# Packing the first five weight tiles by tile of x, and loading x between the weights, at the start of a two-block transformer kernel

## The chip, the core and the metric

The kernel runs on one core of a Trainium2 chip. The metric is the time of one execution on the device in microseconds. Three executions before the change took 1213.05, 1207.31 and 1213.48 us (median 1213.05).

## What is computed

Two blocks follow each other on x of 256 tokens by 1024 channels, in fp32. The change concerns the first lines of the first block alone:

```python
h = rms_norm(x, norm_mix_g[l])          # x * rsqrt(mean(x*x) + 1e-6) * g
proj = h @ w_in[l]
qa, ka, va, qc, kc, vc, rx, rgate, gates = jnp.split(proj, offs, axis=-1)
ya = moba_attention(qa..., ka..., va...)
```

`qa`, `ka` and `va` are 512 columns each. Behind them come a recurrence, a second attention, gated merges, a feed-forward part, and then a second block of two layers, whose code the change leaves as it is.

## The kernel before

**Layout.** x lies transposed: 8 tiles of 128 channels by 256 tokens (`x[:, k]`, k = 0 to 7). A weight tile is 128 x 128 fp32 (64 KB). An output tile of 128 columns needs eight weight tiles, one for each tile of x. All weights of the program are packed on the host, in the order of their use, into one stream that `_plan` writes down (L63 and after); `Stream` (L147) reads it in chunks of eight tiles (512 KB) into six raw buffers. In `_plan` each of the eight `qa` and `ka` output tiles is a run of eight weight tiles, so chunk 0 holds all of `qa` tile 0, chunk 1 all of `qa` tile 1, and so on.

**Splitting.** Products are made from a high and a low part, both in the format that TensorE reads. For a chunk, ScalarE casts to `whi` (L186) and VectorE subtracts to `wlo` (L187); there are five buffers of each. Chunk 0 is split in pieces of 2, 3 and 3 tiles, chunks 1 and 2 in halves. Each weight tile then takes three matmuls of 256 columns (`mm3`, L343 to L345): high with high, high with the low part of the moving operand, low with high.

**The start.** `load_x` (L262) loads two tiles of x at a time. SyncE issues x 0 and 1, two tiles of chunk 0, x 2 and 3, the other six tiles, x 4 to 7, and then chunks 1 to 5 and the tables. Thirteen warm-up matmuls on `ones` (L328) run meanwhile.

**The first projections** go through `seam` (L476) with nothing before it (`prev` is empty). The norm's factor for a token can be applied after the product, so the first `NSTART` = 5 output tiles (four of `qa`, one of `ka`) are computed on x times the gain alone: `zh` and `zl` (registers R0 and R1, L509 and L510). Tile by tile, all eight k are done before the next begins. After the third tile (`i == 2`) the norm is finished: `norm.add` sums squares (L393, L396 on ScalarE, L405 on GpSimd and once on VectorE), `stats` (L418) adds over channels with a matmul against `ones`, VectorE and ScalarE make the reciprocal root (L428, L471 to L474, result `n_r`), and `apply` writes the normalised input for all later tiles: product with `n_r` (L457), high part `hh` (L464, ScalarE), low part `hl` (L465, VectorE). The five tiles are scaled by `n_r` when they leave PSUM (L532). The other `ka` tiles, and all that follows, read `hh` and `hl`: in this document "the key tiles" are these three, `ka` 1 to 3. Behind them `tokens` computes `va` (VA, L759 to L761).

**What sets the order.** A scheduler orders each engine's instructions when the program is built; each engine then runs its own list in order. The lists are shown below where the change moves them.

Of the kernel before, what the change touches and what calls it, by code (L numbers as in the profile page):

```python
# [10 lines left out]
F32 = mybir.dt.float32  # L11
F32R = mybir.dt.float32r
# [54 lines left out]
def _plan():  # L67

    runs = []

    def cols(name, layer, col, nk=8, nc=1):
        runs.append((name, layer, nk, col, nc))

    for c in (QA, KA):
        for m in range(4):
            cols("w_in", 0, c + m * P)
    cols("w_in", 0, VA, 8, 4)
    for m in range(8):
        cols("w_in", 0, RX + m * P)
        if m > 1:  # L80
            runs.append(("rg", 0, 2, m - 2, 1))
        cols("w_in", 0, GT + m * P)
    for c in (QC, KC):
        for m in range(4):
            cols("w_in", 0, c + m * P)
            if c == QC and m < 2:
                runs.append(("rg", 0, 2, 6 + m, 1))
    cols("w_in", 0, VC, 8, 4)
    for m in range(8):
        cols("w_in", 0, RGT + m * P)  # L90
    for m in range(8, 16 + GLEAD):
        cols("w_in", 0, GT + m * P)
    for kind, m in WEAVE:
        if kind == "gate":
            cols("w_in", 0, GT + (16 + m) * P)
        else:
            cols("w_branch_a", 0, m * P, 4)
            cols("w_branch_b", 0, m * P, 8)
            cols("w_branch_c", 0, m * P, 4)
    for m in range(8):  # L100
        cols("w_out", 0, m * P)
    for j in range(FT):
        cols("ffn_up", 0, j * P)
        cols("ffn_up", 0, (j + FT) * P)
    for m in range(8):
        cols("ffn_down", 0, m * P, FT)
    for l in range(2):
        for c in (XC2, GB2):
            for m in range(2):
                cols("w_in_2", l, c + m * P)  # L110
        cols("w_in_2", l, K2)
        cols("w_in_2", l, V2)
        for m in range(4):
            cols("q2", l, m)
        for c in (POOL2, GC2):
            for m in range(2):
                cols("w_in_2", l, c + m * P)
        for n in range(GLEAD2):
            if n == POOLAT:
                runs.append(("pool2", l, 2, 0, 1))  # L120
            cols("w_in_2", l, GT2 + (n % 3 * 8 + n // 3) * P)
        for kind, m in WEAVE2:
            if kind == "gate":
                cols("w_in_2", l, GT2 + (m % 3 * 8 + m // 3) * P)
            else:
                cols("w_branch_a_2", l, m * P, 2)
                cols("w_branch_b_2", l, m * P, 4)
                cols("w_branch_c_2", l, m * P, 2)
        for m in range(8):
            cols("w_o_2", l, m * P)  # L130
        for j in range(FT):
            cols("w_up_2", l, j * P)
            cols("w_up_2", l, (j + FT) * P)
        for m in range(8):
            cols("w_down_2", l, m * P, FT)
    at, t = {}, 0
    for r in runs:
        at[(r[0], r[1], r[3])] = t
        t += r[2] * r[4]
    return runs, at, t  # L140
# [6 lines left out]
class Stream:  # L147
# [13 lines left out]
    def load(self):  # L161
        c = self.loads
        if c >= NCH:
            return
        n = min(CT, NTILES - c * CT) * P
        t = self.pool.tile([P, CT * P], F32, name="raw", tag="raw", bufs=NRAW)
        src = self.src[c * CT * P * P:c * CT * P * P + P * n].rearrange("(p n) -> p n", p=P)
        cut = 2 * P if c == 0 else n
        self.nc.sync.dma_start(t[:, :cut], src[:, :cut])
        if cut < n:  # L170
            self.between[0]()
            self.nc.sync.dma_start(t[:, cut:n], src[:, cut:])
            self.between[1]()
        self.raw[c] = t
        self.loads += 1

# [59 lines left out]
def _build(tc, ctx, ap):  # L236
# [22 lines left out]
    par = const("par", [P, P_N])  # L259
    nc.scalar.dma_start(par[:, :8], ap["par"][:, :8])  # L260

    def load_x(k):  # L262
        nc.sync.dma_start(x[:, k:k + 2], ap["xT"][k * P:(k + 2) * P].rearrange("(k p) t -> p k t", p=P))

    load_x(0)
    W = Stream(nc, wp, ap["wst"], (lambda: load_x(2), lambda: (load_x(4), load_x(6))))
    nc.sync.dma_start(par[:, 8:], ap["par"][:, 8:])
    sinks = const("sinks", [P, 16])
    nc.sync.dma_start(sinks, ap["row"][None, 256:272].to_broadcast([P, 16]))
# [7 lines left out]
    def cs(name):  # L277
        o, w = C_OFF[name]
        return cst[:, o:o + w]
# [52 lines left out]
    def reg(i, dt=F32, shape=(P, NT, S)):  # L332

        return cp.tile(list(shape), dt, name=f"R{i}", tag=f"R{i}", bufs=1)
# [141 lines left out]
    def seam(prev, evac, norm, nxt, zreg, nahead=NAHEAD):  # L476

        ahead, rest = nxt[:nahead], nxt[nahead:]
        width = S + 2 if norm.ln else S
        if nxt:
            zh, zl = (reg(i, F32R, (P, NT, width)) for i in zreg)
            if norm.ln:
                for i, c in enumerate((norm.g, norm.b)):
                    split(zh[:, :, S + i], zl[:, :, S + i], c)
        for m in range(NT):
            if prev:  # L490
                t0, nk, rhs, _ = prev[m]
                if nk == 8 and m < 3:
                    if m == 0:
                        W.begin(t0, 3 * nk)
                        first = [ps() for _ in range(3)]
                        for ks in (range(6), range(6, 8)):
                            for q, (t, _, r, _) in zip(first, prev):
                                for k in ks:
                                    wh, wl = W.get(t + k)
                                    mm3(q[:, :S], wh, wl, r[0][:, k], r[1][:, k], k == 0, k == 7)  # L500
                    p = first[m]
                else:
                    W.begin(t0, nk)
                    p = ps()
                    group(p[:, :S], t0, nk, rhs)
                evac(m, p[:, :S])
            if nxt:
                g = norm.g[:, m:m + 1]
                A.activation(zh[:, m, :S], x[:, m], AF.Copy, scale=g)  # L509
                V.scalar_tensor_tensor(zl[:, m, :S], x[:, m], g, zh[:, m, :S].bitcast(F32), op0=OP.mult, op1=OP.subtract)  # L510
            if prev:
                norm.add(m, not nxt)
        if not nxt:
            norm.stats(True)
            norm.finish(zreg)
            return
        out = []
        for i, mt in enumerate(ahead):
            W.begin(mt["t0"], 8)
            p = ps()  # L520
            out.append(p)
            for k in range(8):
                wh, wl = W.get(mt["t0"] + k)
                mm3(p[:, :width], wh, wl, zh[:, k], zl[:, k], k == 0, k == 7)
            if i == (0 if prev else 2):
                for m in range(0 if prev else NT):
                    norm.add(m)
                norm.stats()
                norm.apply()
        for mt, p in zip(ahead, out):  # L530
            t = mt["into"] if "into" in mt else wrk()
            V.tensor_tensor(t, p[:, :S], norm.rstd, op=OP.mult)  # L532
            if norm.ln:
                gb = tmp("n_gb", [P, 2], 2)
                A.copy(gb, p[:, S:width])
                u = wrk()
                A.activation(u, norm.nmr, AF.Identity, scale=gb[:, 0:1], bias=gb[:, 1:2])
                G.tensor_add(t, t, u)
            if "evac" in mt:
                mt["evac"](t)  # L540
        for i in range(0, len(rest), 2):
            pair = rest[i:i + 2]
            W.begin(pair[0]["t0"], 8 * len(pair))
            pn = [ps() for _ in pair]
            for k in range(8):
                for mt, p in zip(pair, pn):
                    wh, wl = W.get(mt["t0"] + k)
                    mm3(p[:, :S], wh, wl, hh[:, k], hl[:, k], k == 0, k == 7)
            for mt, p in zip(pair, pn):
                mt["evac"](p[:, :S])  # L550

    def to_hi_lo(dst, i, scale=None):
        return lambda p: split(dst[0][:, i], dst[1][:, i], p, scale)

# [164 lines left out]
    def rope_tables():  # L719
# [12 lines left out]
        for sc in (65536.0, 1.0):  # L732
# [9 lines left out]
        V.tensor_scalar(sinT, sinT, cs("sgn"), None, op0=OP.mult)  # L742

    sc64 = 64 ** -0.5
    seam([], None, n0, [dict(t0=AT["w_in", 0, QA + m * P], nk=8, rhs=HX, evac=to_hi_lo(qa, m, cs("qsa")[:, m:m + 1])) for m in range(4)]
         + [dict(t0=AT["w_in", 0, KA + m * P], nk=8, rhs=HX, evac=to_hi_lo(ka, m)) for m in range(2)], (0, 1), NSTART)
    with tc.issue_after(n0.done.ins):
        small()
    phase([dict(t0=AT["w_in", 0, KA + m * P], nk=8, rhs=HX, evac=to_hi_lo(ka, m)) for m in range(2, 4)])

    def tokens(t0, dst):
        def go():
# [419 lines left out]
```

## Time and profile before

| | |
|---|---|
| median of three executions | 1213.05 us |
| lowest and highest | 1207.31 and 1213.48 us |
| the profiled execution | 1208.3 us, of it the span 1206.3 us |
| mean granted TensorE clock over the span | 0.986 of full speed |
| TensorE matmul busy | 97% of the span |
| VectorE, ScalarE, GpSimd busy | 79%, 63%, 20% |
| weights moved | 395 transfers of 512 KB among 212.61 MB in all |

Times in the profile count from the start of the span. A row of the timeline has start, duration, engine, line of the kernel, operation, output and inputs, and in brackets the idle time of the engine before it and what ended it. "PE" is TensorE, "DVE" VectorE, "ACT" ScalarE, "POOL" GpSimd, and "SPq" the queue of SyncE from which transfers are issued. A share of busy time of PE is not a share of its peak, as matmuls overlap.

### The profile page before, as it was taken

How to read it: one execution, taken by the hardware profiler on the slowest of the kernel's cores; microseconds unless marked ns; L12 is line 12 of the kernel's file. 1: busy time of each engine (PE TensorE's matmuls, PEld its weight loads, DVE VectorE, ACT ScalarE, POOL GpSimd, SP SyncE). 2: the span in 40 equal slices, each digit the busy share in tenths (PEclk: the TensorE clock that was granted, in tenths of full speed). 3: DMA queues.
4: the chain of work that ended last, by engine and by line, in shares of the span. 5: the costliest groups of instructions: out<-in, count | busy, mean ns of one | idle time of the engine just before them, and what ended most of it. 6: DMA issues, size and time to landing. Idle time of an engine off the chain costs nothing.

```text
span 1206.3 us, 25236 instructions
## 1 busy us (share of the span) xinstructions
PE 1165.5 (97%) x9928; PEld 1146.3 (95%) x9928; DVE 956.2 (79%) x1767; ACT 763.7 (63%) x1391; POOL 245.0 (20%) x233
## 2 busy tenths in 40 slices
PE   8999999999999999999999999999999998999895
PEld 8999899999999999999998999999999998999895
DVE  7989886797988856886789988757995888977754
ACT  7678566756767645676557766556776565855542
POOL 2022020001122200120023222222420042222122
PEclk9999999999999999999999999999999998999898
DMA  7654445475466665545554566664455554565541
GB/s 284 224 168 155 166 143 168 127 229 189 148 212 202 196 207 192 162 154 175 184 184 142 165 210 203 209 193 148 151 189 177 185 166 135 155 203 185 189 141 35
DMA packets 60486, 212.61 MB, mean 176 GB/s; under 512 B 6864, under 2 KB 9296, under 8 KB 60368
## 3 DMA queue, kind: packets, MB, share of 16 engines
q1 hardware_dynamic: 60080, 210.88, 54.3%
q8 instruction: 77, 1.26, 0.4%
q10 hardware_dynamic: 288, 0.14, 0.1%
q14 instruction: 41, 0.34, 0.1%
HBM read 209.94 MB, written 1.05 MB: 175 GB/s over the span
## 4 chain that ended last, share of the span: by engine, by line
PE 65%; DVE 17%; ACT 9%; issue 5%; POOL 3%; DMA 0%; SPq 0%; POOLq 0%; ACTq 0%; DVEq 0%
PE ps L344 20%; PE ps L343 20%; PE ps L345 20%; DVE wlo L187 7%; ACT whi L186 4%; POOL wrk L929 2%; DVE R L510 1%; DVE wrk L923 1%; DVE wrk L922 1%; ACT a_lg L580 1%; PE ps L563 1%; PE ps L760 1%; PE ps L761 1%; PE ps L759 1%; DVE wrk L454 1%
## 5 line engine op out<-in xcount | busy, mean ns | idle before, releaser
L187 DVE TENSOR_TENSOR wlo<-raw,whi 128x1024 fp32r<-128x1024 f32 (+1 forms) x401 | 496.3, 1240 | 118.5 <-ACT whi L186 113.1
L343 PE MATMUL ps<-hh,whi 128*128 128x256 f32 x1912 | 536.5, 281 | 5.1 <-ACT hh L461 3.6
L344 PE MATMUL ps<-hl,whi 128*128 128x256 f32 x1912 | 532.0, 279 | 3.2 <-DVE hl L462 3.1
L186 ACT CAST whi<-raw 128x1024 fp32r<-128x1024 f32 (+1 forms) x401 | 414.6, 1038 | 186.8 <-PE ps L344 135.5
L345 PE MATMUL ps<-hh,wlo 128*128 128x256 f32 x1912 | 531.3, 278 | 0.6 <-DVE wlo L187 0.4
L343 PEld LDWEIGHTS ps<-hh,whi 128*128 128x128 f32 x1912 | 361.6, 189 | 8.3 <-ACT hh L461 4.0
L344 PEld LDWEIGHTS ps<-hl,whi 128*128 128x128 f32 x1912 | 362.1, 190 | 4.4 <-DVE hl L462 4.0
L345 PEld LDWEIGHTS ps<-hh,wlo 128*128 128x128 f32 x1912 | 361.1, 189 | 1.0 <-DVE wlo L187 1.0
L343 PE MATMUL ps<-R,whi 128*128 128x256 f32 (+1 forms) x1180 | 330.2, 281 | 6.8 <-ACT R L355 3.8
L344 PE MATMUL ps<-R,whi 128*128 128x256 f32 (+1 forms) x1180 | 329.5, 280 | 5.2 <-DVE R L510 3.5
L345 PE MATMUL ps<-R,wlo 128*128 128x256 f32 (+1 forms) x1180 | 327.9, 279 | 0.4 <-DVE wlo L187 0.2
L343 PEld LDWEIGHTS ps<-R,whi 128*128 128x128 f32 x1180 | 223.6, 190 | 9.0 <-ACT R L355 4.5
L344 PEld LDWEIGHTS ps<-R,whi 128*128 128x128 f32 x1180 | 223.5, 189 | 7.5 <-DVE R L510 4.9
L345 PEld LDWEIGHTS ps<-R,wlo 128*128 128x128 f32 x1180 | 223.1, 189 | 1.3 <-DVE wlo L187 1.2
L929 POOL TENSOR_TENSOR wrk<-wrk 128x256 f32<-128x256 f32 x63 | 82.9, 1316 | 238.6 <-DVE wrk L923 150.3
L355 ACT CAST R<-wrk 128x256 fp32r<-128x256 f32 x89 | 36.0, 407 | 117.5 <-POOL wrk L929 95.3
L405 POOL TENSOR_TENSOR n_sq<-n_sq,n_q 128x256 f32<-128x256 f32 x42 | 39.5, 941 | 169.1 <-ACT n_q L396 167.9
L922 DVE SCALAR_TENSOR_TENSOR wrk<-ps,par,wrk 128x255 f32<-128x255 f32 x120 | 56.6, 476 | 17.3 <-ACT wrk L921 17.3
L356 DVE TENSOR_TENSOR R<-wrk,R 128x256 fp32r<-128x256 f32 x89 | 38.9, 440 | 27.0 <-ACT R L355 26.9
L923 DVE SCALAR_TENSOR_TENSOR wrk<-ps,par,wrk 128x254 f32<-128x254 f32 x120 | 57.1, 477 | 1.6
L611 POOL TENSOR_SCALAR a_lg<-a_lg,a_r 128x256 f32<-128x256 f32 x24 | 25.3, 1056 | 113.1 <-DVE a_r L586 60.9
L509 ACT ACTIVATE R<-x,par 128x256 fp32r<-128x256 f32 x48 | 23.8, 507 | 27.8 <-DVE x L889 16.0
(225 smaller groups left out, 1088.7 us busy)
## 6 DMA issues: line engine op xcount, KB each, us to landing
raw<-in_wst SPq DMA_DIRECT2D x395, 512.0 KB, 4.0
x<-in_xT SPq DMA_DIRECT2D x4, 256.0 KB, 4.8
out_y<-x SPq DMA_DIRECT2D x3, 256.0 KB, 2.2
cst<-in_cst SPq DMA_DIRECT2D x1, 406.0 KB, 8.9
raw<-in_wst SPq DMA_DIRECT2D x1, 384.0 KB, 5.5
par<-in_par SPq DMA_DIRECT2D x1, 312.5 KB, 8.5
raw<-in_wst SPq DMA_DIRECT2D x1, 256.0 KB, 2.7
out_y<-x SPq DMA_DIRECT2D x2, 128.0 KB, 2.0
```

The costliest lines, as they stand in the source:

```text
L186: self.nc.scalar.copy(hi[:, a:b], w[:, a:b])
L187: self.nc.vector.tensor_sub(lo[:, a:b], w[:, a:b], hi[:, a:b].bitcast(F32))
L343: T.matmul(out, sh, mh, start=first, stop=False, skip_group_check=skip)
L344: T.matmul(out, sh, ml, start=False, stop=False, skip_group_check=skip)
L345: T.matmul(out, sl, mh, start=False, stop=last, skip_group_check=skip)
L355: A.copy(hi, src)
L356: V.tensor_sub(lo, src, hi.bitcast(F32))
L405: e.tensor_add(self.sq, self.sq, q)
L611: (G if i else V).tensor_scalar(pe[:, c], pe[:, c], r[:, i:i + 1], None, op0=OP.mult)
L922: V.scalar_tensor_tensor(y[:, 1:], p[:, :S - 1], pr(cw, 44 + i), y[:, 1:], op0=OP.mult, op1=OP.add)
L923: V.scalar_tensor_tensor(y[:, 2:], p[:, :S - 2], pr(cw, i), y[:, 2:], op0=OP.mult, op1=OP.add)
L929: G.tensor_tensor(y, held.pop(j), y, op=OP.mult)
```

## The change

The first five output tiles' weights are one run of 40 tiles now, packed by k: the five tiles for x tile 0, the five for x tile 1, and so on. A new function `begin` replaces the call of `seam`: for each k it makes `zh` and `zl` of that tile of x, and then five times three matmuls, one set for each output tile, into five PSUM tiles at once. `norm.add(k)` follows each k; `stats` and `apply` follow the eighth. The loads of x come apart: x 0, five tiles of chunk 0, x 1, the other three, chunk 1, x 2 and 3, chunk 2, x 4 and 5, chunk 3, x 6 and 7, chunks 4 and 5. The three key tiles go through `phase`, one after the other.

```diff
--- before.py
+++ after.py
@@ -71,9 +71,9 @@
     def cols(name, layer, col, nk=8, nc=1):
         runs.append((name, layer, nk, col, nc))
 
-    for c in (QA, KA):
-        for m in range(4):
-            cols("w_in", 0, c + m * P)
+    cols("w_in", 0, QA, 8, NSTART)
+    for m in range(NSTART, 8):
+        cols("w_in", 0, QA + m * P)
     cols("w_in", 0, VA, 8, 4)
     for m in range(8):
         cols("w_in", 0, RX + m * P)
@@ -165,12 +165,13 @@
         n = min(CT, NTILES - c * CT) * P
         t = self.pool.tile([P, CT * P], F32, name="raw", tag="raw", bufs=NRAW)
         src = self.src[c * CT * P * P:c * CT * P * P + P * n].rearrange("(p n) -> p n", p=P)
-        cut = 2 * P if c == 0 else n
+        cut = NSTART * P if c == 0 else n
         self.nc.sync.dma_start(t[:, :cut], src[:, :cut])
         if cut < n:
             self.between[0]()
             self.nc.sync.dma_start(t[:, cut:n], src[:, cut:])
-            self.between[1]()
+        elif c < len(self.between):
+            self.between[c]()
         self.raw[c] = t
         self.loads += 1
 
@@ -259,11 +260,11 @@
     par = const("par", [P, P_N])
     nc.scalar.dma_start(par[:, :8], ap["par"][:, :8])
 
-    def load_x(k):
-        nc.sync.dma_start(x[:, k:k + 2], ap["xT"][k * P:(k + 2) * P].rearrange("(k p) t -> p k t", p=P))
-
-    load_x(0)
-    W = Stream(nc, wp, ap["wst"], (lambda: load_x(2), lambda: (load_x(4), load_x(6))))
+    def load_x(k, n=2):
+        nc.sync.dma_start(x[:, k:k + n], ap["xT"][k * P:(k + n) * P].rearrange("(k p) t -> p k t", p=P))
+
+    load_x(0, 1)
+    W = Stream(nc, wp, ap["wst"], (lambda: load_x(1, 1), lambda: load_x(2), lambda: load_x(4), lambda: load_x(6)))
     nc.sync.dma_start(par[:, 8:], ap["par"][:, 8:])
     sinks = const("sinks", [P, 16])
     nc.sync.dma_start(sinks, ap["row"][None, 256:272].to_broadcast([P, 16]))
@@ -549,6 +550,28 @@
             for mt, p in zip(pair, pn):
                 mt["evac"](p[:, :S])
 
+    def begin(norm, t0, evacs, zreg):
+
+        zh, zl = (reg(i, F32R) for i in zreg)
+        out = [ps() for _ in evacs]
+        n = len(evacs)
+        for k in range(NT):
+            g = norm.g[:, k:k + 1]
+            A.activation(zh[:, k], x[:, k], AF.Copy, scale=g)
+            V.scalar_tensor_tensor(zl[:, k], x[:, k], g, zh[:, k].bitcast(F32), op0=OP.mult, op1=OP.subtract)
+            W.begin(t0 + n * k, n)
+            for i, p in enumerate(out):
+                wh, wl = W.get(t0 + n * k + i)
+                mm3(p[:, :S], wh, wl, zh[:, k], zl[:, k], k == 0, k == 7)
+            norm.add(k)
+            if k == NT - 1:
+                norm.stats()
+                norm.apply()
+        for p, ev in zip(out, evacs):
+            t = wrk()
+            V.tensor_tensor(t, p[:, :S], norm.rstd, op=OP.mult)
+            ev(t)
+
     def to_hi_lo(dst, i, scale=None):
         return lambda p: split(dst[0][:, i], dst[1][:, i], p, scale)
 
@@ -742,11 +765,10 @@
         V.tensor_scalar(sinT, sinT, cs("sgn"), None, op0=OP.mult)
 
     sc64 = 64 ** -0.5
-    seam([], None, n0, [dict(t0=AT["w_in", 0, QA + m * P], nk=8, rhs=HX, evac=to_hi_lo(qa, m, cs("qsa")[:, m:m + 1])) for m in range(4)]
-         + [dict(t0=AT["w_in", 0, KA + m * P], nk=8, rhs=HX, evac=to_hi_lo(ka, m)) for m in range(2)], (0, 1), NSTART)
+    begin(n0, AT["w_in", 0, QA], [to_hi_lo(qa, m, cs("qsa")[:, m:m + 1]) for m in range(4)] + [to_hi_lo(ka, 0)], (0, 1))
     with tc.issue_after(n0.done.ins):
         small()
-    phase([dict(t0=AT["w_in", 0, KA + m * P], nk=8, rhs=HX, evac=to_hi_lo(ka, m)) for m in range(2, 4)])
+    phase([dict(t0=AT["w_in", 0, KA + m * P], nk=8, rhs=HX, evac=to_hi_lo(ka, m)) for m in range(1, 4)])
 
     def tokens(t0, dst):
         def go():
```

**TensorE at the norm's statistics.** `ps` numbers tell output tiles apart, R0 and R1 are `zh` and `zl`. Before, around the end of the third output tile:

```order
L343 MATMUL ps_277<-R0_165,whi_201 128x256
L344 MATMUL ps_277<-R1_166,whi_201 128x256
L345 MATMUL ps_277<-R0_165,wlo_202 128x256
L418 MATMUL ps_325<-n_sq_164,ones_92 128x256
L343 MATMUL ps_374<-R0_165,whi_234 128x256
```

The change, around the same statistics (its lines are one higher, L419 is L418); 490, 523 and 556 are the key tiles:

```order
L345 MATMUL ps_172<-R1_167,whi_225 128x256
L346 MATMUL ps_172<-R0_166,wlo_226 128x256
L419 MATMUL ps_388<-n_sq_165,ones_93 128x256
L344 MATMUL ps_490<-hh_102,whi_271 128x256
L344 MATMUL ps_523<-hh_102,whi_297 128x256
L344 MATMUL ps_556<-hh_102,whi_344 128x256
L345 MATMUL ps_490<-hl_103,whi_271 128x256
```

Before, 72 of the 120 matmuls of the five tiles stood ahead of the statistics and 48 behind; now all 120 stand ahead, and behind comes the first key tile, which reads `hh` and `hl`.

**VectorE from the statistics to the low halves.** Before:

```order
L428 TENSOR_SCALAR wrk<-ps 128x256
L187 TENSOR_TENSOR wlo<-raw,whi 128x1024
L472 TENSOR_TENSOR wrk<-wrk 128x256
L473 SCALAR_TENSOR_TENSOR wrk<-wrk 128x256
L474 SCALAR_TENSOR_TENSOR n_r<-wrk 128x256
L643 TENSOR_SCALAR hb_a<-par 128x8
L644 TENSOR_SCALAR hb_x<-par 128x8
L457 TENSOR_TENSOR wrk<-x,n_r 128x256 x3
L465 SCALAR_TENSOR_TENSOR hl<-wrk,par,hh 128x256 x3
```

The change (L429 is L428, L475 is L474, L458 is L457, L466 is L465, L572 is L532):

```order
L429 TENSOR_SCALAR wrk<-ps 128x256
L188 TENSOR_TENSOR wlo<-raw,whi 128x1024
L473 TENSOR_TENSOR wrk<-wrk 128x256
L474 SCALAR_TENSOR_TENSOR wrk<-wrk 128x256
L188 TENSOR_TENSOR wlo<-raw,whi 128x1024
L475 SCALAR_TENSOR_TENSOR n_r<-wrk 128x256
L666 TENSOR_SCALAR hb_a<-par 128x8
L667 TENSOR_SCALAR hb_x<-par 128x8
L458 TENSOR_TENSOR wrk<-x,n_r 128x256 x6
L466 SCALAR_TENSOR_TENSOR hl<-wrk,par,hh 128x256 x6
L458 TENSOR_TENSOR wrk<-x,n_r 128x256 x2
L572 TENSOR_TENSOR wrk<-ps,n_r 128x256
```

A second subtraction of a chunk stands inside the reciprocal root, six products stand ahead of the first low half instead of three, and an evacuation of a query tile stands ahead of the last two low halves.

**SyncE's first transfers.** Before, and then in the change:

```order
L263 DMA x<-in_xT 128x2x256
L169 DMA raw<-in_wst 128x256
L263 DMA x<-in_xT 128x2x256
L172 DMA raw<-in_wst 128x768
L263 DMA x<-in_xT 128x2x256 x2
L169 DMA raw<-in_wst 128x1024 x5
```

```order
L264 DMA x<-in_xT 128x256
L169 DMA raw<-in_wst 128x640
L264 DMA x<-in_xT 128x256
L172 DMA raw<-in_wst 128x384
L169 DMA raw<-in_wst 128x1024
L264 DMA x<-in_xT 128x2x256
L169 DMA raw<-in_wst 128x1024
L264 DMA x<-in_xT 128x2x256
```

Chunk 1 moves from behind all of x to behind its first two tiles. The number of instructions on TensorE, VectorE, ScalarE and GpSimd is the same in both programs, and from early in VA on their order is too; SyncE has one transfer more.

## Rows read from the trace of the kernel before

**Rows 1.** The page: the span, and busy time, share and instructions by engine.

```profile
span 1206.3 us, 25236 instructions
PE 1165.5 (97%) x9928; PEld 1146.3 (95%) x9928; DVE 956.2 (79%) x1767; ACT 763.7 (63%) x1391; POOL 245.0 (20%) x233
```

**Rows 2.** Busy time by stretch: length, busy us (records) by engine, granted clock, DMA share, GB/s.

```profile
5.35:12.15 6.80, 4.51 (x30) 3.50 (x28) 4.33 (x11) 5.66 (x14) 2.10 (x3) 1.00 1.02 372
12.15:23.79 11.64, 11.64 (x97) 11.44 (x97) 11.00 (x20) 7.45 (x15) 3.74 (x4) 1.00 0.97 382
23.79:33.68 9.89, 9.37 (x74) 8.76 (x73) 9.64 (x21) 9.76 (x18) 0.00 (x0) 1.00 0.46 153
```

**Rows 3.** Timeline of TensorE, the first 9 us: start, duration, what.

```profile
1.03 4.58 PE L328 MATMUL ps<-ones 128*128 128x128 f32 x26 [1.03 <-DVE halfpi L288]
...
8.27 0.38 PE L343 MATMUL ps<-R,whi 128*128 128x256 f32 x1 [1.96 <-ACT whi L186]
```

**Rows 4.** Timeline of ScalarE, 3 to 8.6 us.

```profile
3.68 0.91 ACT L509 ACTIVATE R<-x,par 128x256 fp32r<-128x256 f32 x2 [0.98 <-DMA x<-in_xT]
4.49 0.39 ACT L186 CAST whi<-raw 128x256 fp32r<-128x256 f32 x1
...
5.64 0.91 ACT L509 ACTIVATE R<-x,par 128x256 fp32r<-128x256 f32 x2 [0.44 <-DMA x<-in_xT]
...
7.71 0.93 ACT L186 CAST whi<-raw 128x384 fp32r<-128x384 f32 x2 [0.85 <-DMA raw<-in_wst]
```

**Rows 5.** Timeline of SyncE's queue: the last two tiles of x, then chunks 1 to 5.

```profile
2.69 0.95 SPq L263 DMA_DIRECT2D x<-in_xT  x2
3.68 3.22 SPq L169 DMA_DIRECT2D raw<-in_wst  x5
```

**Rows 6.** Transfers: size, us to landing; of those issued at 2.69, and at 3.68.

```profile
x<-in_xT SPq DMA_DIRECT2D x1, 256.0 KB, 5.6
...
raw<-in_wst SPq DMA_DIRECT2D x1, 512.0 KB, 6.6
```

**Rows 7.** Groups by line and shape, 0 to 34 us: busy us, mean ns.

```profile
L186 ACT CAST whi<-raw 128x1024 fp32r<-128x1024 f32 x10 | 10.2, 1043 | 0.2 <-ACT R L355 0.2
...
L509 ACT ACTIVATE R<-x,par 128x256 fp32r<-128x256 f32 x8 | 3.5, 499 | 1.4 <-DMA x<-in_xT 1.4
...
L396 ACT ACTIVATE n_q<-x 128x256 f32<-128x256 f32 x7 | 2.8, 408 | 0.5 <-POOL n_sq L405 0.5
```

**Rows 8.** Busy time by stretch, 10 to 12.5 us; the last number is GB/s.

```profile
10.00:12.50 2.50, 2.27 (x16) 1.86 (x16) 1.96 (x5) 2.20 (x6) 1.72 (x2) 1.00 1.03 421
```

**Rows 9.** Timeline of the norm: TensorE's statistics, then VectorE to the last low halves.

```profile
17.60 0.70 PE L418 MATMUL ps<-n_sq,ones 128*128 128x256 f32 x2
...
18.60 0.41 DVE L428 TENSOR_SCALAR wrk<-ps 128x256 f32<-128x256 f32 x1
18.94 1.21 DVE L187 TENSOR_TENSOR wlo<-raw,whi 128x1024 fp32r<-128x1024 f32 x1
20.07 0.41 DVE L472 TENSOR_TENSOR wrk<-wrk 128x256 f32<-128x256 f32 x1
...
20.97 0.42 DVE L474 SCALAR_TENSOR_TENSOR n_r<-wrk 128x256 f32<-128x256 f32 x1
...
21.46 1.09 DVE L457 TENSOR_TENSOR wrk<-x,n_r 128x256 f32<-128x256 f32 x3
22.47 1.28 DVE L465 SCALAR_TENSOR_TENSOR hl<-wrk,par,hh 128x256 fp32r<-128x256 f32 x3
...
27.67 0.88 DVE L465 SCALAR_TENSOR_TENSOR hl<-wrk,par,hh 128x256 fp32r<-128x256 f32 x2
```

**Rows 10.** Busy time of TensorE by stretch, 1009 to 1017.8 us: length, busy, granted clock, DMA.

```profile
1009.00:1011.70 2.70, 0.00 (x0) 0.86 0.51 181
1011.70:1014.40 2.70, 1.94 (x7) 0.50 0.03 14
1014.40:1017.80 3.40, 3.40 (x18) 0.50 0.36 82
```

## The prediction

> **What bounds the kernel now.** Start with the page's busy shares: TensorE works through 97% of the span [rows 1], so whatever changes only other engines is worth nothing unless TensorE waits for it. The change touches only what runs until the value projection (VA) begins, so I cut that stretch by TensorE's own events [rows 2]. From the first projection matmul at 5.35 us to 12.15 us, TensorE is busy 4.51 of 6.80 us with 30 records: it waits for data. From 12.15 to 23.79 us it never stops: 97 records in 11.64 us, 0.12 us for a matmul, 0.36 us for a weight tile with its three. From 23.79 to 33.68 us the three key tiles run on the normalised input, busy 9.37 of 9.89 us; then VA starts. So the whole prize is the idle part of 28.33 us (5.35 to 33.68): the work is 64 tiles of three matmuls, 192 x 0.12 = 23.0 us, and 0.35 us for the statistics (half of the 0.70 of two passes that overlap with what follows [rows 9]), which leaves **5.0 us, 0.4% of the span**, as the most that can be won.
>
> The timeline shows the losses. The warm-up matmuls run until 5.61, and the largest wait is 1.96 us for the high half of weights at 8.27 [rows 3]. ScalarE in its turn waits for transfers: x of 256 KB was there at 3.68, 640 KB of the queue at 5.64, 1024 KB at 7.71 [rows 4]. The pair of x issued second from 2.69 on ends 1280 KB [rows 5]; the earlier of that pair landed 5.6 us after its issue, so 1280 KB stand at 8.3 [rows 6]. Chunk 1 (2048 KB) was issued at 3.68 and landed 6.6 us later, at 10.3 [rows 5, 6].
>
> **The change, part by part.**
>
> *Fewer bytes ahead of the first work.* Same tiles, same casts and subtractions, but five output tiles now advance together over one tile of x. Ahead of the first five weight tiles stand 128 + 320 = 448 KB; between the rows for 256 and 640 KB that lands near 4.7, the 0.39 us cast makes it 5.1, and the warm-ups hold TensorE until about 5.35 anyway [rows 3, 4]. So the start does not move. Five tiles take it to 7.2; the other three of chunk 0 (768 KB, near 6.3) are in time, and TensorE has finished all eight near 8.3. Chunk 1 now ends 1280 KB: 8.3 by the row, and half a chunk's cast later (half of 1.04 us), 8.8, TensorE goes on, 0.5 us idle. From there ScalarE owes per chunk one cast (1.04) and two tiles of x (2 x 0.50, 2 x 0.41), 2.9 us, against TensorE's 8 x 0.36 = 2.9 [rows 7]: even, so I add 0.7 us for waits on low halves (chosen: each first use of a piece waits for a subtraction of some 0.5 us, and 0.24 of it runs beside the two matmuls on the high half). The 40 tiles end at 8.8 + 32 x 0.36 + 0.7 = **21.0 us**. Before they and the statistics ended at 23.79; with 0.35 us for the statistics now 21.4, so this part gains 2.4 us. Bounds: with no wait after 5.35 they end at 19.8 (1.2 earlier); if the order in the queue helps nothing and chunk 1 lands at 10.3 as before, 2.0 later.
>
> The Trainium skill ("DMA: Bandwidth & Descriptors", section on the anatomy of one DMA) fits a transfer on the gpsimd path as 2.0 us plus its bytes at 436 GB/s; an estimate by it would have 1280 KB here 5 us after the first issue at the latest, and the sum would end at its lower bound. Our rows disagree with it for the first 8 us (8.3 us for the same bytes) and come near its rate only later: 421 GB/s from 10.0 to 12.5 [rows 8]. I take the rows.
>
> *The norm chain moves behind all 40 tiles.* This is the step that costs. Before, the statistics matmul stood after 24 tiles, at 17.60, and 16 more tiles covered what follows it [rows 9]. Now it stands after the fortieth, and what comes next on TensorE needs the normalised input. VectorE's evacuation follows about 0.7 us after the matmul: 21.7. Before it took 18.60 to 21.39 from there to the end of the reciprocal root, one weight subtraction (18.94 to 20.07, 1.13 us) in between; now two stand there, so 2.79 + 1.13 = 3.9 us: 25.6. The first scaled tile starts 0.49 us after the last step of the root began (20.97 to 21.46), so at 25.7. VectorE's order is then six products, six low halves, two products, one evacuation of a query tile, two low halves: three products took 1.01 us (21.46 to 22.47), three low halves 1.2, hence 2.0 + 2.4 + 0.67 + 0.34 + 0.8 = 6.2 us: the last low half is there at **31.9**, before 28.55 (27.67 + 0.88). ScalarE's casts of later chunks, three of them ahead of the first high half, end near 25.4 and do not delay it.
>
> So TensorE stands from 21.4 until the first high half (about 26.6), then walks through the first key tile at VectorE's pace, and has 72 - 22 - 4 = 46 of the key matmuls left at 31.9: 46 x 0.12 = 5.5 us. VA begins at 37.4 to 37.5 instead of 33.68: **+3.8 us**. Weights for VA are not late: at the same rates VectorE comes to chunk 8 near 35.6 and has it near 36.8.
>
> *Clock.* After 2.70 us without a matmul the granted clock was 0.50 (1.2 of 2.4 GHz) through 6.1 us, 18 matmuls in 3.40 us, 0.19 each [rows 10]. Here the stop is 5 us. If the clock falls, the first key tile takes 24 x 0.19 = 4.6 us instead of VectorE's 3.9 or so: +0.7, which I take. At the other end the slow 6.1 us lie over key tiles that only TensorE limits and cost half of themselves, 3.1; nothing at all is the lower end.
>
> *Issues on SyncE.* x goes in five transfers instead of four, one issue of 0.5 us more; the transfers already issued keep the engines busy meanwhile, so nothing [rows 4, 5]. Chunks 2 to 5 stand behind more of x than before, yet chunk 2 is first used near 12 us and chunk 3 near 15: the bytes in front of them (1536 and 2304 KB) are down before that by the rows for 1280 and 2048 KB, 2 us for 768 KB. From early in VA on every engine's order is the same as before, so I carry the shift through to the end.
>
> **Sum:** +3.8 + 0.7 = **+4.5 us**, bounds 3.8 - 1.2 = +2.6 and 3.8 + 2.0 + 3.1 = +8.9. The profiled execution took 1208.3 us, which gives 1212.8; it lies 4.75 under the median shown (1213.05), and the shown runs go from 1207.31 to 1213.48. I put the shift on the middle of the four known times, (1208.3 + 1213.05) / 2 = 1210.7: **1215.2 us**. A measurement of this kernel tells about 0.5%, 6 us, from no change, so the forecast lies inside "same", on the slow side.
>
> **The rivals.**
>
> *The clock stays low into the second and third key tile* (the side of slower). Place: 26 to 34 us on TensorE; it decides from the point at which the stop, 5 us by my count, draws a low stretch that begins only when the key tiles do. For it: a stop of 2.70 us was enough once [rows 10]. Against: 1.96 us at 8.27 [rows 3] was not, the granted clock was 1.00 through it [rows 2], and part of the low stretch will fall into the idle time. Price 3.8 + 3.1 = +6.9: 1217.6.
>
> *The queue lands no earlier*: transfers overlap so that chunk 1 still arrives at 10.3. For it: many transfers are open at once and could share the engines. Against: each of ScalarE's waits follows the bytes in front [rows 4]. +3.8 + 2.0 + 0.7 = +6.5: 1217.2, slower by a hair.
>
> *The transfers run at their later rate from the start*, so TensorE never waits after 5.35. Rows 8 speak for it, rows 4 against. +2.6 + 0.7 = +3.3: 1214.0. This is the mechanism behind the page's formula above.
>
> *The chain costs nothing*: some later wait takes the delay up, or the key tiles don't need the last low half; 2.4 us gained at best: 1208.3 to 1210.7. Against: TensorE's order puts all 24 matmuls of the first key tile ahead of nearly all others, and no queue is starved at VA.
>
> **How the numbers follow.** Forecast 0.50; clock into the later tiles 0.20; queue no earlier 0.08; steady rate 0.15; chain costs nothing 0.07. The first two rivals are slower by over 0.5%: 0.28. Faster by over 0.5% would need 6 us where 5.0 are to be had, so it gets only 0.03 for the scatter of the runs; same is 0.69. The range is 1208.5 to 1222: from a low run (1207.3) with a shift a little under the lower bound, since the last rival has a chance, to a high one (1213.5) with nearly the upper bound.
>
> **What would show it.** Right: no wait of 1.96 us near 8; 40 tiles done near 21; TensorE idle some 5 us after the statistics matmul; last low half near 32; VA near 37.5; from there the same distances as before. Wrong: statistics that run while query tiles are still in work; VA before 33.7; chunk 1 at 10 us or after; a granted clock of 1.00 all through 20 to 40 us takes 0.7 off, one of 0.50 past 34 us adds up to 3.

## The result and the profile after

| | before | after |
|---|---|---|
| median of 12 executions each | 1207.82 us (1204.53 to 1213.48) | **1216.47 us** (1211.15 to 1222.86) |
| ratio to before, 95% interval | | **1.007** (1.0045 to 1.0094) |
| a second set (31 and 9 executions) | 1212.33 us | 1220.51 us: 1.0059 (1.0024 to 1.0095) |
| profiled execution, its span | 1208.3, 1206.3 us | 1217.45, 1215.7 us |
| first projection matmul, statistics, last low half done, VA | 5.37, 17.60, 28.55, 33.68 us | 6.61, 22.39, 33.18, 39.50 us |

The change is slower by 7 to 9 us. (The ratios, here and below, are estimated from all executions and are not quotients of the two medians.) VA begins 5.8 us later in the profiled executions; over three profiles of each program (33.68, 33.48, 33.27 and 39.50, 39.29, 39.59) it is 6.0 us.

The page's busy shares after, which answer to [rows 1], do not show where it is lost: 4.4 us more busy time on TensorE, as many instructions.

```profile
span 1215.7 us, 25236 instructions
PE 1169.9 (96%) x9928; PEld 1150.3 (95%) x9928; DVE 958.5 (79%) x1767; ACT 763.5 (63%) x1391; POOL 239.0 (20%) x233
```

The stretch up to VA does. Busy time by stretch of the profile after, cut at TensorE's events as in [rows 2] (columns as there): the 40 tiles, the stop behind the statistics, the key tiles.

```profile
6.61:22.39 15.78, 15.20 (x122) 14.43 (x122) 11.67 (x16) 11.35 (x23) 5.89 (x6) 1.00 1.03 393
22.39:27.92 5.53, 0.60 (x4) 0.20 (x3) 4.86 (x11) 3.80 (x6) 0.00 (x0) 0.93 0.68 248
27.92:39.50 11.58, 11.05 (x73) 10.76 (x73) 10.34 (x33) 8.09 (x17) 0.00 (x0) 0.74 0.13 46
```

The five output tiles now run with hardly a break (15.20 of 15.78 us; in [rows 2] 4.51 of 6.80 in the first part). Then TensorE does 0.60 us of work in the 5.53 from the statistics to the first high half, and the key tiles take 11.58 us instead of 9.89, at a mean clock of 0.74. TensorE's timeline around the stop, after:

```profile
22.39 0.60 PE L419 MATMUL ps<-n_sq,ones 128*128 128x256 f32 x2
27.92 1.00 PE L344 MATMUL ps<-hh,whi 128*128 128x256 f32 x3 [4.93 <-ACT hh L465]
29.45 0.58 PE L345 MATMUL ps<-hl,whi 128*128 128x256 f32 x1 [0.53 <-DVE hl L466]
29.83 0.41 PE L346 MATMUL ps<-hh,wlo 128*128 128x256 f32 x1
30.05 0.41 PE L344 MATMUL ps<-hh,whi 128*128 128x256 f32 x1
30.26 0.41 PE L345 MATMUL ps<-hl,whi 128*128 128x256 f32 x1
```

The wait of 4.93 us ends with the first high half; from 29.45 on the matmuls start 0.21 us apart instead of 0.12. VectorE's timeline over the same stretch, after, is the norm's chain of [rows 9], one step behind the other:

```profile
23.03 0.42 DVE L429 TENSOR_SCALAR wrk<-ps 128x256 f32<-128x256 f32 x1 [2.33 <-PE ps L419]
23.37 1.22 DVE L188 TENSOR_TENSOR wlo<-raw,whi 128x1024 fp32r<-128x1024 f32 x1
24.50 0.42 DVE L473 TENSOR_TENSOR wrk<-wrk 128x256 f32<-128x256 f32 x1
24.95 0.42 DVE L474 SCALAR_TENSOR_TENSOR wrk<-wrk 128x256 f32<-128x256 f32 x1
25.30 1.22 DVE L188 TENSOR_TENSOR wlo<-raw,whi 128x1024 fp32r<-128x1024 f32 x1
26.43 0.42 DVE L475 SCALAR_TENSOR_TENSOR n_r<-wrk 128x256 f32<-128x256 f32 x1
...
26.91 2.09 DVE L458 TENSOR_TENSOR wrk<-x,n_r 128x256 f32<-128x256 f32 x6
28.93 2.45 DVE L466 SCALAR_TENSOR_TENSOR hl<-wrk,par,hh 128x256 fp32r<-128x256 f32 x6
31.30 0.75 DVE L458 TENSOR_TENSOR wrk<-x,n_r 128x256 f32<-128x256 f32 x2
31.97 0.41 DVE L572 TENSOR_TENSOR wrk<-ps,n_r 128x256 f32<-128x256 f32 x1
32.31 0.87 DVE L466 SCALAR_TENSOR_TENSOR hl<-wrk,par,hh 128x256 fp32r<-128x256 f32 x2
```

The second subtraction at 25.30 stands inside the root, as the order said. From the statistics to the last low half it is 10.8 us, against 10.95 before [rows 9]: the chain has not grown, only its cover is gone.

The clock over the same time, by stretch, after:

```profile
20.00:27.00 7.00, 2.99 (x24) 2.59 (x22) 4.63 (x10) 4.21 (x5) 0.00 (x0) 1.00 0.80 308
27.10:33.90 6.80, 5.45 (x24) 5.16 (x25) 6.80 (x20) 3.81 (x9) 0.00 (x0) 0.50 0.28 98
33.90:39.50 5.60, 5.60 (x51) 5.60 (x50) 4.36 (x17) 4.84 (x9) 0.00 (x0) 1.00 0.02 4
```

The granted clock falls to 0.50 (1.2 of 2.4 GHz) at 27.1, when TensorE has stood for some 4.1 us, and is back at 33.9. In these 6.8 us it begins 24 of the 72 matmuls of the key tiles, and 48 are left (a row counts a matmul that runs across its edge in both stretches).

### The profile page after: what moved, and what is told of

The parts are those of the page before. It is cut to its first block, busy times and chain, and to the rows that moved or that the text cites. A ratio compares the mean times of both kernels' runs of the same rounds, so it can differ in the third digit from the quotient of the medians.

```text
span 1215.7 us, 25236 instructions
## 1 busy us (share of the span) xinstructions
PE 1169.9 (96%) x9928; PEld 1150.3 (95%) x9928; DVE 958.5 (79%) x1767; ACT 763.5 (63%) x1391; POOL 239.0 (20%) x233
## 4 chain that ended last, share of the span: by engine, by line
PE 68%; DVE 16%; ACT 9%; issue 5%; POOL 2%; DMA 1%; SPq 0%; ACTq 0%; POOLq 0%; DVEq 0%
PE ps L345 21%; PE ps L344 21%; PE ps L346 21%; DVE wlo L188 6%; ACT whi L187 3%; DVE R L511 1%; POOL wrk L951 1%; DVE wrk L945 1%; PE ps L782 1%; PE ps L586 1%; PE ps L783 1%; PE ps L781 1%; DVE wrk L944 1%; DVE R L357 1%; ACT x L456 1%
## 5 line engine op out<-in xcount | busy, mean ns | idle before, releaser
L951 POOL TENSOR_TENSOR wrk<-wrk 128x256 f32<-128x256 f32 x63 | 75.6, 1199 | 247.5 <-DVE wrk L945 196.6
L634 POOL TENSOR_SCALAR a_lg<-a_lg,a_r 128x256 f32<-128x256 f32 x24 | 25.8, 1076 | 117.4 <-DVE a_r L609 61.3
L405 POOL TENSOR_TENSOR n_s<-x 128x256 f32<-128x256 f32 x4 | 4.8, 1198 | 169.9 <-DVE x L911 155.7
```

Source lines behind the costliest of these rows:

```text
L634: (G if i else V).tensor_scalar(pe[:, c], pe[:, c], r[:, i:i + 1], None, op0=OP.mult)
L951: G.tensor_tensor(y, held.pop(j), y, op=OP.mult)
```

## Experiments

Theory: what costs is the place of the statistics. Behind them nothing is left that TensorE could do on x alone, so it waits for the norm's chain, and the clock falls on top. The rivals were that packing by tile of x or the order of loads costs, and that the loss sits elsewhere than in the start.

**fill18: the clock alone.** Eighteen dummy matmuls on a constant keep TensorE at work behind the statistics.

```diff
             if k == NT - 1:
                 norm.stats()
+                busy = ps()
+                for _ in range(NFILL):
+                    T.matmul(busy[:, :P], ones, ones, start=True, stop=True)
                 norm.apply()
```

> The change with 18 more matmuls on the matrix of ones, put behind the statistics, where TensorE stands for 4.93 us; their results are used by nothing. Theory A with its clock term: at about 0.11 us a pass and two passes each they take 4 us and fit into the gap; the granted clock stays 1.00 through 20 to 40 us, the first key tile runs at VectorE's pace, VA begins 0.7 to 1.2 us earlier relative to the statistics matmul (16.0 to 16.4 us after it instead of 17.1), the time falls by about 1 us against the change. Rival (the low clock is hidden by VectorE's pace): VA begins 17.1 us after the statistics as in the change, no gain. Second rival (the filling matmuls hold up the key tiles): VA later than 17.3 us after the statistics.

TensorE's timeline of fill18:

```profile
22.04 0.60 PE L420 MATMUL ps<-n_sq,ones 128*128 128x256 f32 x2
22.47 4.18 PE L572 MATMUL ps<-ones 128*128 128x128 f32 x36
27.57 0.61 PE L345 MATMUL ps<-hh,whi 128*128 128x256 f32 x3 [0.92 <-ACT hh L466]
29.10 0.39 PE L346 MATMUL ps<-hl,whi 128*128 128x256 f32 x1 [0.92 <-DVE hl L467]
...
37.18 0.63 PE L785 MATMUL ps<-whi,hh 128*128 128x512 f32 x2
```

The first high half comes as late after the statistics as in the change (5.53 us in both), and the chain is as long (10.8 us), but no row has a low clock before 645 us. After the last low half 38 matmuls are left before VA instead of 52, and VA follows it by 4.36 us instead of 6.32: the clock costs **2.0 us** (2.0 to 2.4 against the three profiles of the change, which have 6.32, 6.73 and 6.48). That is more than the 0.7 to 1.2 us that I expected. VA still stands 3.7 us behind the mean of before (33.48): that is the uncovered chain, less what the start gained. The whole took 1218.55 us, a ratio of 1.0056 (1.0024 to 1.0088); 2 us cannot be told in the time of the whole.

**warm8: the late start.** The first projection matmul came at 6.61 instead of 5.37, behind warm-ups that lasted to 6.86 in this profile instead of 5.61 [rows 3]. Eight warm-ups in place of thirteen.

```diff
-NWARM = 13
+NWARM = 8
```

> The change with 8 warm-up matmuls instead of 13. In the change the first projection matmul started at 6.61 us, behind the last warm-up (3.76 to 6.87), although its weights were there at 5.2. If the warm-ups hold TensorE up, it starts at 5.2 to 5.4 now and the 40 tiles end up to 1.2 us earlier (statistics at 21.2 to 21.6 instead of 22.39), the time falls by about 1 us. Rival (the transfers set the pace of all 40 tiles, the start does not matter): statistics at 22.2 to 22.5 as before, no gain. Second rival (with fewer warm-ups the clock is still low at 5.3): matmuls of 0.21 us at the start, statistics later than 22.5.

TensorE's timeline of warm8:

```profile
4.86 0.58 PE L344 MATMUL ps<-R,whi 128*128 128x256 f32 x1
...
22.22 0.60 PE L419 MATMUL ps<-n_sq,ones 128*128 128x256 f32 x2
28.30 0.80 PE L344 MATMUL ps<-hh,whi 128*128 128x256 f32 x2 [5.49 <-ACT hh L465]
```

The first matmul comes 1.75 us earlier, the statistics 0.17, less than they differ between the change's own profiles (21.77 to 22.39). The late start costs nothing: the weights' way to TensorE sets the 40 tiles. VA came at 38.69, 0.8 us earlier, but not through the start. The scheduler had put VectorE's list behind the statistics in another order (both subtractions behind the root, the low halves after every three products), so the first high half came 6.08 us after the statistics instead of 5.53; and the low clock lay earlier, from 25.8 to 32.6 us, which left 45 matmuls at the last low half instead of 52. The whole took 1215.0 us (1.0029, 0.9999 to 1.0058).

**mix3: cover back behind the statistics.** Three output tiles go by tile of x, the other two of the five each by itself behind them; 72 matmuls stand ahead of the statistics and 48 behind, as before. Chunk 0 is cast in parts of three tiles. The loads are not quite the change's: x 2 and 3 go ahead of chunk 1 here, and x 4 to 7 ahead of chunk 2.

```diff
-NSTART = 5
+NSTART = 3
...
+        for t1, ev in after:
+            W.begin(t1, 8)
+            p = ps()
+            out.append(p)
+            for k in range(NT):
+                wh, wl = W.get(t1 + k)
+                mm3(p[:, :S], wh, wl, zh[:, k], zl[:, k], k == 0, k == 7)
...
-    begin(n0, AT["w_in", 0, QA], [to_hi_lo(qa, m, cs("qsa")[:, m:m + 1]) for m in range(4)] + [to_hi_lo(ka, 0)], (0, 1))
+    begin(n0, AT["w_in", 0, QA], [to_hi_lo(qa, m, cs("qsa")[:, m:m + 1]) for m in range(3)], (0, 1),
+          [(AT["w_in", 0, QA + 3 * P], to_hi_lo(qa, 3, cs("qsa")[:, 3:4])), (AT["w_in", 0, KA], to_hi_lo(ka, 0))])
```

> The change with three output tiles side by side instead of five, and the other two after them, tile by tile as before, so that the norm's statistics stand after 24 weight tiles again, with 16 tiles behind them. Theory A (the loss is the norm chain that nothing covers, 4.93 us of standing TensorE, and the low clock after it): the standing goes, the granted clock stays 1.00 through 20 to 40 us, the early gain of the packing stays; VA begins at 31.5 to 33.5 us instead of 39.50, the time is 1.0 us under to 1 us over that of the kernel before. Theory B (most of the loss lies later, in the stretch from 310 to 484 us where matmuls follow each other in 0.1178 us instead of 0.1133, brought about by the new start): VA begins as early, but the slow stretch comes again and the time stays 5 us or more over that of before.

Busy time by stretch of mix3, cut as above:

```profile
5.52:16.85 11.33, 10.44 (x76) 8.98 (x74) 10.00 (x16) 10.35 (x23) 4.77 (x6) 1.00 1.01 382
16.85:22.85 6.00, 6.00 (x50) 5.95 (x51) 5.93 (x14) 2.30 (x6) 0.00 (x0) 1.00 1.02 409
22.85:32.73 9.88, 9.34 (x74) 8.66 (x73) 9.64 (x27) 9.84 (x18) 0.00 (x0) 1.00 0.52 167
```

TensorE is busy through all 6.00 us behind the statistics, the clock stays at 1.00, and VA begins at 32.73, 0.75 us ahead of the mean of before (33.48). So packing by tile of x and this order of loads cost nothing by themselves; the place of the statistics does. (The change's own order of loads is undone in xfirst.) The whole took 1211.15 us, a ratio of 0.9985 (0.9952 to 1.0017); the change had 1.0059 (1.0024 to 1.0095) against the same executions of before, and the two intervals do not touch. It is the best version of this study, and it can't be told from before.

**mix4 and mix4fill: half the cover, then the clock taken out.** Four tiles go by tile of x and one behind: 96 matmuls ahead of the statistics, 24 behind. In mix4fill ten dummies follow those 24. Against mix3 (the tables of tiles go with NSTART; of x, 2 and 3 go ahead of chunk 1, 4 and 5 ahead of chunk 2, 6 and 7 ahead of chunk 3):

```diff
-NSTART = 3
+NSTART = 4
...
+        busy = ps()
+        for _ in range(NFILL):
+            T.matmul(busy[:, :P], ones, ones, start=True, stop=True)
```

> Four output tiles packed by tile of x, the fifth done by itself behind them: 96 matmuls ahead of the statistics, 24 behind (the change has 120 and 0, mix3 72 and 48). Theory (the norm's chain of 10.9 us must be covered by matmuls on x; what stands behind the statistics covers it): statistics near 19.5, last low half near 30.4, TensorE idle about 2.2 us before the first key matmul instead of 4.9, VA near 34.8 if the granted clock stays at 1.00, near 36.8 if it falls; so +1.1 to +3.1 us at VA against before. Rival (packing by tile of x itself costs, wherever the statistics stand): VA at 37 or later with a clock of 1.00. In the time of the whole: within 0.4% of before, not to be told from it.

> mix4 with ten dummy matmuls on a constant behind the fifth output tile, so that TensorE does not stop there. Two things are asked. (1) The clock at the start: in mix4 the granted clock was 0.50 from 25.0 to 31.8 us and VA began 6.07 us after the last low half; in the change with dummies it stayed at 1.00 and that distance was 4.36. If the clock alone makes this difference, it is 4.3 to 4.6 here and VA is at 34.8 to 35.2; if the key tiles are held up by something else, VA stays at 36.3 or later. (2) The spacing of 0.118 us between about 300 and 480 us: the five profiles that had a clock of 0.50 at 25 to 35 us all showed it there, the four without did not. If the two hang together, this profile shows 0.113 us there; if it is chance, either may be seen.

TensorE's timeline of mix4:

```profile
23.31 0.51 PE L345 MATMUL ps<-hh,whi 128*128 128x256 f32 x2 [0.64 <-ACT hh L466]
25.64 0.58 PE L346 MATMUL ps<-hl,whi 128*128 128x256 f32 x1 [1.83 <-DVE hl L467]
```

Busy time of mix4 by stretch:

```profile
22.10:25.00 2.90, 1.07 (x8) 0.67 (x6) 2.90 (x9) 2.64 (x7) 0.00 (x0) 0.99 0.79 318
25.00:31.80 6.80, 6.16 (x29) 6.17 (x30) 6.80 (x18) 3.99 (x6) 0.00 (x0) 0.50 0.52 153
31.80:36.50 4.70, 4.70 (x43) 4.70 (x43) 1.72 (x6) 2.86 (x6) 0.00 (x0) 1.00 0.11 38
```

And of mix4fill:

```profile
22.10:25.00 2.90, 2.90 (x28) 2.85 (x26) 2.90 (x9) 2.26 (x6) 0.00 (x0) 1.00 0.81 322
25.00:31.80 6.80, 6.33 (x53) 6.17 (x52) 6.80 (x18) 4.77 (x7) 0.00 (x0) 1.00 0.47 142
31.80:36.50 4.70, 3.20 (x25) 2.72 (x24) 4.34 (x17) 4.68 (x11) 0.00 (x0) 1.00 0.11 44
```

TensorE's timeline of mix4fill, in VA:

```profile
36.08 0.51 PE L795 MATMUL ps<-wlo,hh 128*128 128x512 f32 x1 [1.50 <-DVE wlo L190]
```

The statistics came at 19.33 in both and the last low half was done at 30.50 and 30.49, as forecast (30.4). In mix4 there are two stops, 0.64 and 1.83 us with two matmuls between them, and the clock fell at 25.0, inside the second: 29 matmuls against 53 in the same 6.8 us; VA began at 36.57 and 33.96. The clock costs 2.6 us here. Without it VA stands 0.5 us behind the mean of before, earlier than forecast: the last low half left 30 matmuls to do, not fill18's 38. VA itself then stopped 1.5 us for a weight's low half in both, as it does not in before, so this cover is worth less than its start says: 47 matmuls into VA, mix4fill is 2.1 us behind the mean of before. The whole took 1219.34 us (1.0035, 0.9995 to 1.0076) and 1215.96 us (1.0041, 0.9999 to 1.0082).

**xfirst: the loads of before.** The change's packing with x ahead of chunk 1.

```diff
-        elif c < len(self.between):
-            self.between[c]()
+            self.between[1]()
...
-    load_x(0, 1)
-    W = Stream(nc, wp, ap["wst"], (lambda: load_x(1, 1), lambda: load_x(2), lambda: load_x(4), lambda: load_x(6)))
+    load_x(0)
+    W = Stream(nc, wp, ap["wst"], (lambda: load_x(2), lambda: (load_x(4), load_x(6))))
```

> The change with the loads of before: x 0 and 1, five tiles of chunk 0, x 2 and 3, the other three tiles, x 4 to 7, then chunk 1. What is undone is the second half of the change, chunk 1 ahead of the last six tiles of x. Theory (the 40 tiles end when the weights have come, and the prediction's gain is in that order): chunk 1 lands near 10.3 instead of 8.9, the 40 tiles end 0.7 to 1.4 us later, statistics at 22.8 to 23.6 and VA at 39.8 to 41. Rival (ScalarE and VectorE, which make the high and low parts, set the pace, whichever comes first): statistics at 21.8 to 22.4 as in the change, VA at 38.9 to 39.5.

TensorE's timeline of xfirst:

```profile
10.63 0.41 PE L343 MATMUL ps<-R,whi 128*128 128x256 f32 x1 [1.45 <-ACT whi L186]
...
23.24 0.60 PE L418 MATMUL ps<-n_sq,ones 128*128 128x256 f32 x2
28.77 0.79 PE L343 MATMUL ps<-hh,whi 128*128 128x256 f32 x2 [4.94 <-ACT hh L464]
```

Busy time of xfirst by stretch:

```profile
10.85:14.27 3.42, 3.42 (x18) 3.42 (x18) 3.42 (x4) 3.42 (x9) 2.81 (x4) 0.50 1.03 411
```

Chunk 1's first cast starts at 9.97 instead of 8.94 and TensorE waits 1.45 us for it. Statistics come at 23.24, 0.85 to 1.5 us later than in the change's three profiles (22.39, 21.77, 22.32) and about 1.1 us later than their mean; VA came at 39.93, 0.5 us behind theirs. The theory holds: the change's order of loads costs nothing, it gains. But the 1.1 us are not the order alone. Behind the wait the granted clock was 0.50 from 10.85 to 14.27 us, 18 matmuls, where the change had 1.00. What is plain is that TensorE went on with chunk 1 at 10.63 instead of 9.62; what the order is worth at an equal clock is not shown. It is the smaller part of the story.

**after2, after3, before2, before3: what lies behind VA.** The same two programs, profiled again; after2 was timed too (table above). From VA to the end the profiles of before have 1172.7, 1172.2 and 1180.8 us, those of the change 1176.2, 1180.0 and 1176.4. Two things differ from profile to profile there: low stretches of the clock, and a spacing of matmuls that takes one of two values (last section). How much of the scatter each makes is not shown.

> The change again, unaltered, for a second profile and more times. Theory A: VA begins between 38 and 40 us again (the first start of TensorE may differ by up to 1.3 us with the warm-ups). Theory B: matmuls are spaced 0.1178 us in the stretch from 310 to 484 us again. If that slow stretch is chance, it is gone or lies elsewhere, and the span is then 1207 to 1211 us.

> The kernel before, unaltered, profiled once more. The 256-column matmuls followed each other either every 0.113 us or every 0.118 us, at a granted clock of 1.00 in both, over stretches of 100 to 170 us; the second spacing was seen in the profiles of the change and of its variants and not in the one profile of before. Chance theory: the spacing is drawn anew in each execution, so that this profile of before holds a stretch of 0.118 us too, somewhere, of 50 us or longer, and its span may come out 2 to 6 us over 1206.3. Rival: the change brings it about; then before shows 0.113 us in all its long unstalled stretches again and a span within 2 us of 1206.3. The start should be as it was: VA within 0.3 us of 33.68.

> The kernel before, unaltered, profiled a third time, for the spacing of the matmuls alone. If a clock of 0.50 at 25 to 35 us and the spacing of 0.118 us at 300 to 480 us hang together, this profile has 0.113 us there (no low clock near 30 us in either profile of before); stretches of 0.118 us elsewhere are expected from chance. If it is chance everywhere, about every other profile has it.

> The changed kernel, unaltered, profiled a third time: if the two hang together, a clock of 0.50 near 27 to 34 us and a spacing of 0.118 us from about 300 to 480 us, as in both profiles so far; if it is chance, one in two. VA at 39.2 to 39.6.

Busy time from 310 to 460 us, one row for a profile: before, after, before3, after3.

```profile
310.00:460.00 150.00, 150.00 (x1326) 150.00 (x1325) 118.51 (x179) 95.66 (x153) 32.78 (x25) 1.00 0.63 200
```

```profile
310.00:460.00 150.00, 150.00 (x1276) 150.00 (x1275) 119.08 (x182) 95.20 (x153) 24.70 (x24) 1.00 0.58 189
```

```profile
310.00:460.00 150.00, 150.00 (x1276) 150.00 (x1275) 116.16 (x175) 93.37 (x150) 25.47 (x25) 1.00 0.62 193
```

```profile
310.00:460.00 150.00, 150.00 (x1326) 150.00 (x1325) 120.85 (x186) 97.50 (x157) 32.80 (x25) 1.00 0.64 197
```

1326 or 1276 matmuls in 150 us, at a clock of 1.00 in all four. The first two rows alone had suggested that the change brings the slower spacing about, and the first nine profiles that it goes with a low clock near 27 us (five with both, four with neither). mix4fill, the tenth, had neither. The last two rows show that neither idea is a rule: before3 has the slower spacing there without the low clock, after3 the low clock without the slower spacing, and before2 had it elsewhere (773 to 856 and 1018 to 1136 us). Over all twelve profiles, five of the six with the low clock have the slower spacing here and one of the six without. Whether the low clock makes it likelier is open, and with it whether some of the change's price behind VA is this.

## Why the prediction was right, and where it was not

The time, 1216.47 us, lies 1.3 us over the forecast and well inside the range; the mechanism is the one that was forecast. That the time came so near is luck. I put the shift on 1210.7 us, and the twelve executions of before have a median of 1207.82, 2.9 us lower; the shift was +8.6 us where I had +4.5. The two errors nearly cancel (in the second set before stood at 1212.33 and the shift was +7.2). The ratio of 1.007 lies beyond the 0.5% that I called "same" and gave 0.69, though its interval reaches down to 1.0045; the forecast itself lay close to that line.

- *Start at 5.35.* Wrong, 6.61, but without effect (warm8).
- *40 tiles at 21.0.* Too early by 1.4 us: this is the term that was mis-sized. Chunk 1 was cast from 8.94 on, where I had its bytes at 8.3; TensorE went on at 9.62 instead of 8.8. The other 96 matmuls took 12.8 us to the statistics against 32 x 0.36 + 0.7 = 12.2: waits such as 0.21 us for a low half at 10.34. The gain was there, 2.4 us less 1.4, and xfirst, without the new order of the queue, came 1.1 us later, with a low clock in it; how much of the gain is the order's is not shown. My lower bound did not come true: 1280 KB took until 8.9, and DMA moved 281 GB/s from 3.5 to 8.5 us (400 from 8.5 to 22.4). The Trainium skill ("DMA: Bandwidth & Descriptors", section on the anatomy of one DMA) had supported that bound with 2.0 us plus bytes at 436 GB/s, a fit for the gpsimd path; these transfers, issued from SyncE, did not follow it.

```profile
3.50:8.50 5.00, 5.00 (x33) 5.00 (x32) 2.41 (x5) 2.42 (x7) 0.54 (x1) 1.00 0.85 281
8.50:22.40 13.90, 13.32 (x108) 12.55 (x107) 11.10 (x14) 10.51 (x21) 5.35 (x6) 1.00 1.04 400
```

- *The norm's chain behind all 40 tiles.* Right: 10.8 us from the statistics to the last low half (10.9 forecast), TensorE standing 4.93 us (5). That VectorE's list, read row by row, gave this was worth more than any total. One reading in it was off: I had VectorE's evacuation 0.7 us behind the statistics, where rows 9 have 1.0 (17.60 to 18.60); it came 0.64 us behind, so the error did no harm.
- *What is left at the last low half.* 46 matmuls at 0.12 plus 0.7 for the clock made 6.2 us; measured 6.32. Two errors cancel: without the clock's fall 38 matmuls are left, 4.36 us, and the clock costs 2.0, not 0.7. I had priced the low clock against VectorE's pace through the first key tile alone. But TensorE, at 0.21 us a matmul (I had taken 0.19), fell behind the low halves, and what it had not done stayed to be done: 52 matmuls instead of 38.
- *Shift carried through from VA.* As a mean it holds: +6.0 us at VA, +8.6 us (5.4 to 11.4) and +7.2 us (2.9 to 11.5) in the two sets. What lies between them is not resolved; in single profiles the part behind VA differs by up to 8.6 us within one program.
- *Rivals.* The queue lands no earlier: no, xfirst shows the difference. Steady rate from the start: no. The chain costs nothing: no. The clock into the second and third key tile: its place was wrong, the low stretch ended about where the first tile did (24 matmuls to 33.9), but its price was nearer than my own (2.0 against 3.1 and 0.7).

## What to carry to other kernels

Feeding several outputs from each arriving tile makes a start denser, but it also puts all independent work ahead of the reduction that everything later waits for. Keep as much independent work behind the reduction as its chain needs to the first result that the next work can use (here 5.5 us to the first high half in the change, 6.2 before): 48 matmuls, 6.0 us, were enough; with 24 VA came 3.1 us later than before, with none 6.0. And read the chain from the order of the slowest engine, row by row. Price a low clock by the backlog that it leaves, not by the instructions that run in it.

## What the runs showed of the hardware that was not expected

The 256-column matmuls in this format follow each other every 0.1133 us or every 0.1178 us at a granted clock of 1.00, over stretches of 100 us and more: 1326 or 1276 in 150 us, as above. The long stretches began at a stall of 0.2 us or more and ended at one or where the spacing became uneven, and the same program shows either. At 4.5 ns a matmul such a stretch costs 6 us (50 matmuls more to do at 0.118), as much as the whole change. The Trainium skill ("TensorE: Matmul & The Clock Gate", section on the back-to-back issue gap) says that weight load and matmul set the spacing together, some 81 ns for 128 columns and 131 ns for 512. Both values here, for 256 columns, lie between these, but the 512-column matmuls of VA start 0.23 us apart at a clock of 1.00 (39.50, 39.73 and 39.95 us in the change), so the figure for 512 does not hold in this kernel. No run shows what selects between the two spacings.

In these traces the length of a stop alone does not say whether the clock falls. A single stop of 1.45 us in xfirst was followed by a clock of 0.50, from 10.85 to 14.27 us; a single one of 1.96 us in the profile of before was not [rows 3]. In mix4 the clock fell at 25.0, after a stop of 0.64 us and two matmuls, 1.2 us into a stop of 1.83. In the long stop behind the statistics it fell 3.0 us after TensorE's last work in warm8, and 4.1, 5.0 and 4.5 us after it in the three profiles of the change.
